# First layer of a long network on one Trainium2 core: sums of weights with a vector moved from GpSimd and VectorE to TensorE

## The chip, the cores and the metric

One program runs on one core of a Trainium2 chip. The metric is the device time of one execution in microseconds (us); less is better. The engines are TensorE (PE in the profile; PEld is its loading of weights), VectorE (DVE), ScalarE (ACT), GpSimd (POOL) and SyncE (SP, which here issues the DMAs). Each takes its own instructions in order and waits for the others by semaphores.

## The reference

A network over 512 tokens of width 1024, in float32. Only its first layer matters here, for the latents x and for a context ctx of 256 tokens:

```python
s_lat, s_ctx = silu(c), silu(c_ctx)                        # vectors of 1024
mod_l = split(s_lat @ ada_w[0] + ada_b[0], 6)              # shift, scale, gate; shift, scale, gate
mod_c = split(s_ctx @ ada_w[0] + ada_b[0], 6)
a_lat = rmsnorm(x, norm1_g[0]) * (1 + mod_l[1]) + mod_l[0]
a_ctx = rmsnorm(ctx, norm1_g[0]) * (1 + mod_c[1]) + mod_c[0]
p_lat = a_lat @ mix_w_in + mix_b_in                        # q, k, v and the hyena columns
kv_ctx = a_ctx @ mix_w_in[:, 512:1536] + mix_b_in[512:1536]
att = differential_attention(q, [k_ctx, k], [v_ctx, v])    # 4 heads, 512 queries, 768 keys
hy = x0 * long_conv(v * x1)                                # from the hyena columns
x = x + mod_l[2] * (concat(att, hy) @ mix_w_out + mix_b_out)
x = x + mod_l[5] * (relu(modulate(rmsnorm(x), mod_l[3], mod_l[4]) @ w1) ** 2 @ w2)
```

Behind it come a second layer (pooling and another MLP) and two layers of another kind (recurrence, attention, gated feed-forward).

## The kernel before

**Products.** Features lie on the partitions, tokens on the free axis. Every large product is made of three passes in a fast float32 form: weights and inputs are each split into a rounded part h and a remainder l, and `mm3` (lines 456 to 460) adds wh·xh, wl·xh and wh·xl into a PSUM bank. A tile of the product over 1024 rows is 24 matmuls of 128x512.

**Stream of weights.** Weights arrive in parts of 512 KB in a ring of six `raw` buffers (`_dma_to`, L233). `_emit_h` makes h on ACT (L255) and `_emit_l` makes l on DVE or POOL (L273); then the buffer is free, and SP issues the DMA of the part six places on. `consume` hands out a part for a product, and before it returns calls `prefetch(look)`, which emits the splits of the parts beyond. Parts of the modulation weights `ada_w` (kind "ada") are mixed into this stream; they are not split. `plan` (L742) sets the order: behind the last k part two such parts, behind the pairs of `qh` parts 4, 2, 4, 2, 4, 4 and 2.

**Sums of weights with a vector.** The vectors of modulation are sums over the rows of `ada_w`, each row times an entry of `s_lat`. `_ada_step` (L386) multiplies each raw 128x512 block by a scalar per partition on POOL (L371) or ACT (L373) and adds it on POOL (L383) to an accumulator; when the eight blocks of a half are through, DVE transposes and reduces (`ada_sums`, L416 and L418), and `flush` puts the entries on their partitions by TensorE (L426). A half is 512 of the 6144 entries; halves 0 and 1 are the first shift, 2 and 3 the scale, 4 to 11 the rest.

**Order of the first layer.** `start` (0 to about 140 us) computes V of x and ctx from inputs times gains, in eight steps k; the gains are small TensorE products (`strip`, L1007). `first_shift` sums halves 0 and 1 for x and for ctx, a part at a time beside the steps k (`fstep`): half 0 on POOL, half 1 on DVE (L369, L378) and on ACT with POOL. The sums over the partitions are 32 TensorE instructions (L1096), and the shift `sh` follows (L1099). Then the normed inputs A and AC are made (L1112 to L1136). `layer0` goes on with q (one tile), four k tiles for x and ctx (about 130 to 184 us), and 16 steps s of attention (to about 375 us). In each step the scores of 128 queries (L1492, L1497), the softmax, the combination of two components (L1519, L1520), transposes (L1533) and the product with V stand beside one tile of the `qh` columns. The long convolution and the output product end the layer's mixing at about 475 us. `v_shift`, run in steps beside the k tiles and the first attention steps, multiplies the raw V weights by the shift: for x on DVE (L369, L378), for ctx on ACT and POOL (L373, L383), then a TensorE sum over the partitions (L1161).

**PSUM.** Six banks (`ps`) serve the products and two (`pss`) the small ones: strips, transposes, sums.

Of the kernel before, what the change touches and what calls it, by code (L numbers as in the profile page):

```python
# [11 lines left out]
F32 = mybir.dt.float32  # L12
# [42 lines left out]
class Weights:  # L55
    """h and l views of one part, by chunk of the contraction"""
# [9 lines left out]
# which engine takes which small operation, and the order of the steps that run beside each other  # L66
# [10 lines left out]
    ada='GGAGGA',  # L77
    fs='GGVA',
    vs='VA',
    fstep=(1, 2, 1, 0, 0, 1, 0, 3),  # L80
# [29 lines left out]
    vsj=(2, 1, 0, 1),  # L110
    fj=(1, 2, 0, 2),
    vs1=(0, 1, 1, 1, 1, 1, 1, 1, 1, 1, 1, 1, 1, 1, 1, 1),
    vs2=(1, 1, 0, 3, 1, 1, 1, 1, 1, 1, 1, 1, 1, 1, 1, 1),
# [22 lines left out]
class Prog:  # L136
    def __init__(self, tc, ctx, a, out, tap=None):
# [23 lines left out]
        self.look = LOOK  # L161
        self.l_eng = self.V
# [33 lines left out]
    def piece(self, label, src, parts):  # L196
        """src: dram view, rows x blocks x columns; parts: (kind, which blocks and columns of the view, extra), each loaded alone"""
        for kind, (k, n), extra in parts:
            p = dict(label=label, src=src[:, k, n], raw=None)
            self.pieces.append(p)  # L200
            self.parts.append((p, (kind, extra)))

    def wpiece(self, label, w, k0, kc, n0, nc_, by_k=False, shift=None):
        """shift: (layer, which) of the shift whose product with the weights is wanted besides"""
# [112 lines left out]
    def prefetch(self, n_ahead):  # L317
        """splits emitted up to n_ahead weight parts beyond the one consumed last"""
# [23 lines left out]
    def consume(self, label):  # L342
# [15 lines left out]
        self.prefetch(self.look)  # L358
        return W

# [5 lines left out]
    def scaled(self, mode, out, x, sc):  # L366
        """out = x * sc, by the vector engine, by GpSimd or by the scalar engine"""
        if mode == "V":
            self.V.tensor_scalar(out, x, sc, None, op0=ALU.mult)  # L369
        elif mode == "G":  # L370
            self.G.tensor_scalar(out, x, sc, 0.0, op0=ALU.mult, op1=ALU.add)  # L371
        else:
            self.S.activation(out, x, AF.Copy, scale=sc)  # L373

    def add_scaled(self, mode, out, x, sc):
        """out += x * sc, by the vector engine, by GpSimd or by the scalar engine and GpSimd"""
# [9 lines left out]
    def _ada_step(self, p, layer, half, i):  # L386
        raw = p["raw"]
        s = self.s_lat if layer < 2 else self.col("c_2", 0, 8)
        mode = (PR["ada"][half - 4] if layer == 0 and 4 <= half < 10 else self.ada_mode)
# [14 lines left out]

    def ada_tick(self, want=None):
        """the rest of sums that came ready a while ago, or of those wanted"""
# [14 lines left out]
    def flush_into(self, out, src):  # L421
        """A column of ada_r holds 32 entries, each as the sums over the four quarters of the partitions: add these up
        and put each entry on its partition."""
# [4 lines left out]
    def flush(self, layer):  # L428
        """the modulation vectors that are ready"""
# [32 lines left out]
    def gemm(self, label, x, n_tiles, evac, outer=0, looks=None):  # L462
        """x: list of (h, l) tiles, one for each 128 of the contraction; evac(m, psum)"""
# [38 lines left out]
    def steps(self, gen):  # L502
        """one step of the generator with each tick"""
# [10 lines left out]
    def gemm1(self, label, xs):  # L514
# [4 lines left out]
        for k, x in enumerate(xs):  # L519
            self.mm3(ps[:], w[k], x, k == 0, k == len(xs) - 1)  # L520
        self.put(w.tiles)
# [73 lines left out]
    def head_x(self, k):  # L595
        """x times the norm's gains, ahead of the norm"""
# [8 lines left out]
    def head(self, chain, gs, sh, evac):  # L605
        """The first four tiles of a product with a norm's output start from x times the gains; the factor of each token
        and the product with the shift come on behind. chain() gives the factors. Returns the norm's output."""
# [43 lines left out]
    def norm_mod(self, xs, bc, gs, sh, n=T, free=False, each=None):  # L651
        """h/l pairs of x * rstd * gs + sh"""
# [32 lines left out]
    def gain(self, name, layer, i, g=None, width=8):  # L685
        """g * (1 + scale) as columns"""
# [9 lines left out]
    def sin_red(self, x, out, P, tmp, quarter=False):  # L696
        """out = sin(x), or cos(x); x is kept. In steps"""
# [84 lines left out]
    # parts split ahead by the last products before a norm: the head's parts are through before the last ones  # L782
# [73 lines left out]
    def hyena_filter(self, hd, w3):  # L856
        """Spectrum of the filter, in steps. With t and f both even or odd the transform falls into four of half the size:
        frequency 511 - f has the cosine and sine of f, but for signs that go by the parity of t."""
# [47 lines left out]
    def hyena_hidden(self, z, w1, w2, w3):  # L906
        """hidden layers of the filter's network, in steps"""
# [23 lines left out]
    def first_shift(self):  # L931
        """sums over the rows of the first layer's weights for the shifts of x and ctx, in steps"""
        for half in range(2):
            acc = [self.get(), self.get()]
            for i in range(4):
                p = self.parts[self.cur][0]
                self.cur_h = self.cur_l = self.cur = self.cur + 1
                for kk in range(2):
                    k = 2 * i + kk
                    for c, o in enumerate(acc):  # L940
                        sc, w = self.s2[:, k, c:c + 1], p["raw"][:, kk, :]
                        if k == 0:
                            self.scaled(PR["fs"][2 * half + c], o[:], w, sc)
                        else:
                            self.add_scaled(PR["fs"][2 * half + c], o[:], w, sc)
                self._done_part(p)
                if i == 3:
                    self.first_acc.append(acc)
                yield

    # steps of the filter's hidden layers, and strips of the gains, beside each part of V
# [3 lines left out]
    def start(self):  # L955
        """V of x and ctx, tokens on the partitions, from the tokens times the norm's gains: the factor of each token is put
        on it, the product with the shift is left to v_shift. Besides, the first layer's normalised inputs."""
# [38 lines left out]
        gg, sh = c.tile([128, 8, 2], F32, name="gg"), c.tile([128, 8, 2], F32, name="sh")  # L996
        b1 = c.tile([128, 8], F32, name="b1")
# [3 lines left out]
        hidden, shift, self.first_acc = self.hyena_hidden(z, w1, w2, w3), self.first_shift(), []  # L1001

        def strip(k):
            """128 of the gains of x and ctx, in steps"""
# [86 lines left out]
        ps = self.ps_s.tile([128, 512], F32, tag="pss", name="pss")  # L1091
        for half, acc in enumerate(self.first_acc):
            for c_, o in enumerate(acc):
                for k in range(4):
                    j = 8 * c_ + 4 * half + k
                    PE.matmul(ps[:, j:j + 1], lhsT=o[:, k * 128:(k + 1) * 128], rhs=self.ones[:, 0:1], start=True, stop=True)  # L1096
            self.put(acc)
        for c_ in range(2):
            V.tensor_tensor(sh[:, :, c_], ps[:, 8 * c_:8 * c_ + 8], self.col("ada_b", 0, 8), op=ALU.add)  # L1099
# [40 lines left out]
        self.sh = sh  # L1140
# [5 lines left out]
    def v_shift(self):  # L1146
        """V's products with the shifts, in steps; then V's parts"""
        V, G, S = self.V, self.G, self.S
        acc = [self.get(), self.get()]
        for k in range(8):  # L1150
            for c, o in enumerate(acc):
                if k == 0:
                    self.scaled(PR["vs"][c], o[:], self.vw[k][:], self.sh[:, k, c:c + 1])
                else:
                    self.add_scaled(PR["vs"][c], o[:], self.vw[k][:], self.sh[:, k, c:c + 1])
            self.put(self.vw[k])
# [1244 lines left out]
```

## Time and profile before

| | us |
|---|---|
| median of 3 runs (lowest, highest) | 2698.91 (2698.41, 2698.95) |
| span of the profiled execution | 2697.1 |
| PE, DVE, ACT, POOL busy | 2487.8, 1863.4, 1106.0, 1567.3 |
| mean granted TensorE clock | 0.952 |

The span is that of the profiled execution, from its first to its last instruction; the runs' median lies 1.8 us above it. Clock 1.00 is TensorE's higher level, 2.4 GHz; 0.50 is 1.2 GHz. A busy PE need not be PE at its peak, and a matmul's recorded duration includes its drain; the distance between two starts shows its cost in a stream.

### The profile page before, as it was taken

What the parts mean: (1) busy time and instruction counts of PE and PEld (TensorE: products, weight loads), DVE (VectorE), ACT (ScalarE), POOL (GpSimd) and SP (SyncE); (2) the same over time, 40 slices, a digit from 0 to 9 for tenths busy, and PEclk for the clock granted to TensorE, in tenths of its full rate; (3) what the DMA queues carried; (4) which work ended last, traced back from release to release, by engine and by line L of the source; (5) the groups of instructions that cost most, each with busy time, mean ns of one, the idle gap of its engine ahead of it and who ended that gap; (6) DMA issues with size and microseconds to landing.
All of it is one profiled execution on the core that took longest, in us unless ns stands there. A gap on an engine that the chain in (4) does not pass through costs nothing.

```text
span 2697.1 us, 32008 instructions
## 1 busy us (share of the span) xinstructions
PE 2487.8 (92%) x11472; PEld 2068.4 (77%) x11472; DVE 1863.4 (69%) x2612; ACT 1106.0 (41%) x2057; POOL 1567.3 (58%) x1250
## 2 busy tenths in 40 slices
PE   7787778999989899999879999999999799999998
PEld 6665667787868688888668887888877688788887
DVE  6899988776666787766888667455477876733334
ACT  3446553433223433334466543222245654423231
POOL 6687756699981689963675348778146744400001
PEclk8788989999989899999889999999999899999999
DMA  7233332366673167662312235666422123233331
GB/s 244 83 118 102 109 94 86 95 191 199 200 218 97 51 177 210 213 177 72 96 57 67 87 92 164 182 192 201 117 75 81 49 81 117 71 102 94 95 91 50
DMA packets 433368, 330.30 MB, mean 122 GB/s; under 512 B 11799, under 2 KB 365207, under 8 KB 433208
## 3 DMA queue, kind: packets, MB, share of 16 engines
q1 hardware_dynamic: 429976, 322.22, 39.8%
q0 software_dynamic: 3232, 6.03, 0.7%
q8 instruction: 90, 1.47, 0.2%
q14 instruction: 70, 0.57, 0.1%
HBM read 319.82 MB, written 8.39 MB: 122 GB/s over the span
## 4 chain that ended last, share of the span: by engine, by line
PE 52%; DVE 8%; POOL 3%; ACT 2%; issue 2%; POOLq 0%; DVEq 0%; ACTq 0%
PE ps L458 16%; PE ps L460 16%; PE ps L459 16%; PE ps L477 2%; PE ps L619 1%; POOL slot L273 1%; DVE slot L1973 1%; POOL slot L664 1%; DVE slot L1925 1%; DVE slot L2038 1%; DVE slot L1961 1%; DVE slot L527 1%; PE ps L2029 0%; DVE slot L682 0%; PE pss L574 0%
## 5 line engine op out<-in xcount | busy, mean ns | idle before, releaser
L458 PE MATMUL ps<-slot 128*128 128x512 f32 (+2 forms) x3120 | 1209.2, 388 | 56.0 <-DVE slot L527 16.8
L460 PE MATMUL ps<-slot 128*128 128x512 f32 (+2 forms) x3120 | 1202.8, 386 | 45.8 <-DVE slot L682 24.7
L459 PE MATMUL ps<-slot 128*128 128x512 f32 (+2 forms) x3120 | 1200.8, 385 | 16.6 <-DVE slot L273 13.5
L458 PEld LDWEIGHTS ps<-slot 128*128 128x128 f32 x3120 | 603.4, 193 | 174.1 <-DVE slot L527 19.6
L460 PEld LDWEIGHTS ps<-slot 128*128 128x128 f32 x3120 | 602.4, 193 | 169.0 <-DVE slot L682 32.7
L459 PEld LDWEIGHTS ps<-slot 128*128 128x128 f32 x3120 | 602.9, 193 | 128.9 <-DVE slot L273 15.2
L255 ACT CAST slot<-raw 128x512 fp32r<-128x512 f32 (+1 forms) x764 | 425.8, 612 | 339.6 <-DMA raw<-in_mlp_w_dram 220.2
L383 POOL TENSOR_TENSOR slot<-slot 128x512 f32<-128x512 f32 x336 | 489.9, 1458 | 57.9 <-ACT slot L373 30.5
L273 DVE TENSOR_TENSOR slot<-raw,slot 128x512 fp32r<-128x512 f32 (+1 forms) x554 | 486.9, 922 | 36.7 <-ACT slot L255 32.0
L542 POOL TENSOR_TENSOR slot<-slot 128x512 f32<-128x512 f32 (+1 forms) x64 | 88.0, 1380 | 555.7 <-ACT slot L536 550.1
L273 POOL TENSOR_TENSOR slot<-raw,slot 128x512 fp32r<-128x512 f32 (+1 forms) x210 | 307.7, 1490 | 141.0 <-ACT slot L255 100.1
L371 POOL TENSOR_SCALAR slot<-raw,cols 128x512 f32<-128x512 f32 x192 | 206.1, 1076 | 58.0 <-DMA raw<-in_w_ada_dram 39.7
L371 POOL TENSOR_SCALAR slot<-raw,s_lat 128x512 f32<-128x512 f32 x144 | 154.9, 1079 | 6.4 <-DMA raw<-in_ada_w_dram 6.3
L619 PE MATMUL ps<-slot 128*128 128x512 f32 x576 | 145.5, 412 | 7.4 <-DVE slot L1812 7.4
L2187 DVE TENSOR_TENSOR slot<-slot,ps 128x512 f32<-128x512 f32 x40 | 27.5, 687 | 175.5 <-PE ps L460 175.5
L536 ACT ACTIVATE slot<-slot 128x512 f32<-128x512 f32 (+1 forms) x98 | 55.3, 575 | 214.4 <-DVE slot L1708 61.4
L619 PEld LDWEIGHTS ps<-slot 128*128 128x128 f32 x576 | 114.0, 200 | 32.5 <-DVE slot L1812 8.3
L526 ACT CAST slot<-slot 128x512 fp32r<-128x512 f32 x80 | 47.1, 619 | 190.0 <-DVE slot L2187 155.8
L664 POOL TENSOR_SCALAR slot<-slot,g,mod 128x512 f32<-128x512 f32 x48 | 57.2, 1198 | 85.8 <-DVE slot L658 85.8
L527 DVE TENSOR_TENSOR slot<-slot 128x512 fp32r<-128x512 f32 x75 | 81.7, 1110 | 35.7 <-ACT slot L526 35.7
L2212 DVE SCALAR_TENSOR_TENSOR slot<-ps,mod,slot 128x512 f32<-128x512 f32 x40 | 30.0, 749 | 102.2 <-PE ps L460 102.2
L416 DVE STREAM_TRANSPOSE slot<-slot 128x512 f32<-128x512 f32 x44 | 31.1, 706 | 94.7 <-POOL slot L383 94.6
(322 smaller groups left out, 2796.7 us busy)
## 6 DMA issues: line engine op xcount, KB each, us to landing
raw<-in_mlp_w_dram SPq DMA_DIRECT2D x128, 512.0 KB, 4.8
raw<-in_w_ada_dram SPq DMA_DIRECT2D x96, 512.0 KB, 4.4
raw<-in_ada_w_dram SPq DMA_DIRECT2D x88, 512.0 KB, 5.0
raw<-in_w_ffn_in_dram SPq DMA_DIRECT2D x88, 512.0 KB, 4.2
raw<-in_w_in_dram SPq DMA_DIRECT2D x56, 512.0 KB, 3.8
raw<-in_w_ffn_out_dram SPq DMA_DIRECT2D x32, 512.0 KB, 5.3
raw<-in_mix_w_dram SPq DMA_DIRECT2D x20, 512.0 KB, 3.9
raw<-in_w_out_dram SPq DMA_DIRECT2D x16, 512.0 KB, 4.1
```

Of the source, the lines that this page charges most:

```text
L255: self.S.copy(r(v), src[:, k:k + kk, :])
L273: eng.tensor_tensor(r(lv), src, v, op=ALU.subtract)
L371: self.G.tensor_scalar(out, x, sc, 0.0, op0=ALU.mult, op1=ALU.add)
L383: self.G.tensor_tensor(out, out, v, op=ALU.add)
L458: self.PE.matmul(out, lhsT=wh, rhs=xh, start=start, stop=False)
L459: self.PE.matmul(out, lhsT=wl, rhs=xh, start=False, stop=False)
L460: self.PE.matmul(out, lhsT=wh, rhs=xl, start=False, stop=stop)
L527: (eng or self.V).tensor_tensor(r(l)[:, 0:n], src, h[:, 0:n], op=ALU.subtract)
L536: self.S.activation(sq[:, 0:n], x, AF.Square, scale=scale)
L542: (eng or self.G).tensor_tensor(st["acc"][:, 0:n], st["acc"][:, 0:n], sq[:, 0:n], op=ALU.add)
L619: PE.matmul(ps[:], lhsT=w[i][:, m * 128:(m + 1) * 128], rhs=r(x[j])[:], start=(k == 0 and n == 0), stop=(k == 7 and n == 2))
L664: self.G.tensor_scalar(y[:, 0:n], t[:, 0:n], gs[:, k:k + 1], sh[:, k:k + 1], op0=ALU.mult, op1=ALU.add)
```

## The change

The sums of the first layer with a vector are computed by TensorE in plain float32 from the raw blocks: a raw block is the stationary operand (128 columns at a time), the vector one or two moving columns. This holds for the first shift (halves 0 and 1), for halves 4 to 9, and for V's product with the shift, where the shift, broadcast to 128 columns, is stationary and the raw V weights move. In the first layer `prefetch` is called behind the matmuls of the product that consumed a part, not ahead of them. `fetch_late` ends where the output product begins. The orders `fstep`, `vsj` and `vs2` change with it; docstrings and comments are taken out.

```diff
-    ada='GGAGGA',
-    fs='GGVA',
-    vs='VA',
-    fstep=(1, 2, 1, 0, 0, 1, 0, 3),
+    fstep=(0, 1, 1, 0, 2, 2, 2, 0),
-    vsj=(2, 1, 0, 1),
+    vsj=(0, 1, 0, 1),
-    vs2=(1, 1, 0, 3, 1, 1, 1, 1, 1, 1, 1, 1, 1, 1, 1, 1),
+    vs2=(0, 1, 0, 3, 1, 1, 1, 1, 1, 1, 1, 1, 1, 1, 1, 1),
...
+        self.fetch_late = True
...
         W = p["hl"].pop(id(part))
         self.cur += 1
-        self.prefetch(self.look)
+        if not self.fetch_late:
+            self.prefetch(self.look)
         return W
+
+    def fetch(self):
+
+        if self.fetch_late:
+            self.prefetch(self.look)
...
     def _ada_step(self, p, layer, half, i):
         raw = p["raw"]
         s = self.s_lat if layer < 2 else self.col("c_2", 0, 8)
-        mode = (PR["ada"][half - 4] if layer == 0 and 4 <= half < 10 else self.ada_mode)
+        if layer == 0 and half < 10:
+            m, b = self.mod[0][:, half * 4:half * 4 + 4], self.col("ada_b", half * 4, 4)
+            ps = self.columns(raw, self.s_lat, 2 * i, 1)
+            self.V.tensor_tensor(m, ps, b if i == 0 else m, op=ALU.add)
+            if i == 3:
+                self.ready.add((layer, half))
+            return
+        mode = self.ada_mode
...
+    def columns(self, raw, vec, k0, n):
+
+        ps = self.ps_s.tile([128, 512], F32, tag="pss", name="pss")
+        for j in range(4):
+            for kk in range(2):
+                self.PE.matmul(ps[:, n * j:n * j + n], lhsT=raw[:, kk, j * 128:(j + 1) * 128],
+                               rhs=vec[:, n * (k0 + kk):n * (k0 + kk) + n], start=(kk == 0), stop=(kk == 1))
+        return ps[:, 0:4 * n]
...
@@ gemm1
             self.mm3(ps[:], w[k], x, k == 0, k == len(xs) - 1)
+        self.fetch()
         self.put(w.tiles)
...
     def first_shift(self):
+        s2 = self.s2[:].rearrange("p k c -> p (k c)")
+        for c in range(2):
+            self.V.tensor_copy(self.sh[:, :, c], self.col("ada_b", 0, 8))
         for half in range(2):
-            acc = [self.get(), self.get()]
+            o = self.sh[:, 4 * half:4 * half + 4, :].rearrange("p k c -> p (k c)")
             for i in range(4):
                 p = self.parts[self.cur][0]
                 self.cur_h = self.cur_l = self.cur = self.cur + 1
-                for kk in range(2):
...
+                self.V.tensor_tensor(o, o, self.columns(p["raw"], s2, 2 * i, 2), op=ALU.add)
                 self._done_part(p)
-                if i == 3:
-                    self.first_acc.append(acc)
                 yield
...
@@ start, behind the eight steps
-        ps = self.ps_s.tile([128, 512], F32, tag="pss", name="pss")
-        for half, acc in enumerate(self.first_acc):
...
-                    PE.matmul(ps[:, j:j + 1], lhsT=o[:, k * 128:(k + 1) * 128], rhs=self.ones[:, 0:1], start=True, stop=True)
-            self.put(acc)
-        for c_ in range(2):
-            V.tensor_tensor(sh[:, :, c_], ps[:, 8 * c_:8 * c_ + 8], self.col("ada_b", 0, 8), op=ALU.add)
...
     def v_shift(self):
-        acc = [self.get(), self.get()]
-        for k in range(8):
-            for c, o in enumerate(acc):
...
-        for c, o in enumerate(acc):
-            ps = self.ps_s.tile([128, 512], F32, tag="pss", name="pss")
-            self.PE.matmul(ps[:], lhsT=self.ones[:], rhs=o[:], start=True, stop=True)
-            V.tensor_tensor(o[:], ps[:], self.bv[:], op=ALU.add)
+        V, acc = self.V, []
+        for c in range(2):
+            ps, o = self.ps_s.tile([128, 512], F32, tag="pss", name="pss"), self.get()
+            for k in range(8):
+                self.PE.matmul(ps[:], lhsT=self.sh[:, k, c:c + 1].to_broadcast([128, 128]), rhs=self.vw[k][:],
+                               start=(k == 0), stop=(k == 7))
+            V.tensor_tensor(o[:], ps[:], self.bv[:], op=ALU.add)
+            acc.append(o)
+            if c == 0:
+                yield
+        self.put(self.vw)
         self.put(self.bv)
...
@@ layer0, the k tiles
                 self.mm3(pc[:, 0:TC], w[k], acs[k], k == 0, k == 7)
+            self.fetch()
...
-        self.look = 0
+        self.look, self.fetch_late = 0, False
```

## Rows read from the trace of the kernel before

**Rows 1.** Busy time by stretch: length, each engine, clock, DMA share, GB/s.
```profile
0.00:88.30 88.30, 69.44 (x307) 57.25 (x308) 65.55 (x97) 29.17 (x56) 56.83 (x51) 0.86 0.64 215
88.30:99.30 11.00, 6.46 (x40) 6.13 (x39) 7.16 (x8) 5.12 (x10) 4.72 (x3) 0.68 0.56 164
...
130.10:184.40 54.30, 42.49 (x201) 35.28 (x202) 53.64 (x67) 26.87 (x47) 46.01 (x32) 0.85 0.35 114
184.40:240.70 56.30, 39.11 (x164) 31.11 (x164) 50.53 (x71) 31.90 (x71) 38.28 (x31) 0.83 0.24 77
240.70:304.00 63.30, 56.60 (x284) 46.77 (x284) 60.88 (x103) 36.94 (x89) 47.71 (x42) 0.93 0.42 133
304.00:375.00 71.00, 56.46 (x286) 47.45 (x284) 63.41 (x111) 43.86 (x97) 36.48 (x28) 0.93 0.29 89
375.00:440.00 65.00, 47.05 (x258) 41.16 (x259) 57.85 (x97) 21.37 (x41) 48.25 (x36) 0.84 0.28 90
```

**Rows 2.** What PE waited for, 130.1 to 304 us: total, times, longest.
```profile
PE pss L1533 <- DVE slot L1520: 13.2, 3, 10.5
```

**Rows 3.** POOL's groups by line, 130.1 to 304 us: busy us, mean ns.
```profile
L383 POOL TENSOR_TENSOR slot<-slot 128x512 f32<-128x512 f32 x40 | 59.5, 1487 | 11.5 <-ACT slot L373 8.5
L371 POOL TENSOR_SCALAR slot<-raw,s_lat 128x512 f32<-128x512 f32 x30 | 31.2, 1043 | 0.0
```

**Rows 4.** DVE in order of time, one operation before and beside POOL's sums.
```profile
20.62 0.42 DVE L700 TENSOR_SCALAR slot<-slot 64x512 f32<-64x512 f32 x1
...
41.11 1.37 DVE L700 TENSOR_SCALAR slot<-slot 64x512 f32<-64x512 f32 x1
```

**Rows 5.** DVE's groups by line and shape, 140 to 200 us.
```profile
L378 DVE SCALAR_TENSOR_TENSOR slot<-slot,sh 128x512 f32<-128x512 f32 x7 | 9.6, 1372 | 0.2
```

**Rows 6.** The same, 200 to 310 us.
```profile
L416 DVE STREAM_TRANSPOSE slot<-slot 128x512 f32<-128x512 f32 x4 | 2.8, 702 | 0.0
L418 DVE TENSOR_REDUCE ada_r<-slot 128x16 f32<-128x512 f32 x4 | 2.7, 685 | 0.1
```

**Rows 7.** All engines in order of time, 76 to 135 us: start, length.
```profile
88.04 7.50 DVE L378 SCALAR_TENSOR_TENSOR slot<-raw,s,slot 128x512 f32<-128x512 f32 x6
...
91.54 3.46 POOL L273 TENSOR_TENSOR slot<-raw,slot 128x512 fp32r<-128x512 f32 x2 [0.68 <-ACT slot L255]
...
95.59 3.58 PE L1096 MATMUL pss<-ones,slot 128*128 128x1 f32 x16 [4.08 <-DVE slot L378]
...
100.23 4.32 POOL L1122 TENSOR_SCALAR slot<-slot,gg,sh 128x512 f32<-128x512 f32 x2 [5.23 <-DVE slot L1112]
```

**Rows 8.** PE in order of time, 190 to 194.5 us.
```profile
191.50 1.88 PE L1161 MATMUL pss<-slot,ones 128*128 128x512 f32 x4
192.82 1.49 PE L1492 MATMUL ps<-slot 128*128 128x512 f32 x4
```

**Rows 9.** PE in order of time, 1600 to 1618 us: a norm's sums inside a head.
```profile
1605.96 1.84 PE L574 MATMUL pss<-ones,slot 128*128 128x1 f32 x16
1607.66 1.03 PE L629 MATMUL pss<-ones,slot 128*128 128x1 f32 x8
1608.55 3.03 PE L619 MATMUL ps<-slot 128*128 128x512 f32 x12
```

**Rows 10.** The same in another head, 1252 to 1276 us.
```profile
1259.74 3.84 PE L574 MATMUL pss<-ones,slot 128*128 128x1 f32 x32
1263.44 1.84 PE L629 MATMUL pss<-ones,slot 128*128 128x1 f32 x8
1265.15 5.17 PE L619 MATMUL ps<-slot 128*128 128x512 f32 x12
```

**Rows 11.** PE's busy time and granted clock in that head, by us.
```profile
1262.00:1263.00 1.00, 1.00 (x11) 1.00 0.00 0
1263.00:1264.00 1.00, 1.00 (x7) 0.50 0.00 0
```

**Rows 12.** The page's DMA issues: KB each, us to landing.
```profile
raw<-in_ada_w_dram SPq DMA_DIRECT2D x88, 512.0 KB, 5.0
```

More of the change, by code (lines that the diff above doesn't have):

```diff
@@ L937, in first_shift @@
                 self.cur_h = self.cur_l = self.cur = self.cur + 1
-                for kk in range(2):
-                    k = 2 * i + kk
-                    for c, o in enumerate(acc):
[L941 to L945, printed above, removed]
+                self.V.tensor_tensor(o, o, self.columns(p["raw"], s2, 2 * i, 2), op=ALU.add)
                 self._done_part(p)
-                if i == 3:
-                    self.first_acc.append(acc)
                 yield
@@ L996, in start @@
         gg, sh = c.tile([128, 8, 2], F32, name="gg"), c.tile([128, 8, 2], F32, name="sh")
+        self.sh = sh
         b1 = c.tile([128, 8], F32, name="b1")
@@ L1000, in start @@
         gx, gc, ws = [], [], []
-        hidden, shift, self.first_acc = self.hyena_hidden(z, w1, w2, w3), self.first_shift(), []
+        hidden, shift = self.hyena_hidden(z, w1, w2, w3), self.first_shift()
         def strip(k):
@@ L1090, in start @@
         S.copy(rc[:, 0:TC], bp[:, 0:TC])
-        ps = self.ps_s.tile([128, 512], F32, tag="pss", name="pss")
-        for half, acc in enumerate(self.first_acc):
-            for c_, o in enumerate(acc):
-                for k in range(4):
-                    j = 8 * c_ + 4 * half + k
-                    PE.matmul(ps[:, j:j + 1], lhsT=o[:, k * 128:(k + 1) * 128], rhs=self.ones[:, 0:1], start=True, stop=True)
-            self.put(acc)
-        for c_ in range(2):
-            V.tensor_tensor(sh[:, :, c_], ps[:, 8 * c_:8 * c_ + 8], self.col("ada_b", 0, 8), op=ALU.add)
         self.vt = []
@@ L1139, in start @@
         self.put(rc)
-        self.sh = sh
         self.put(cxt)
@@ L1146, in v_shift @@
     def v_shift(self):
-        V, G, S = self.V, self.G, self.S
-        acc = [self.get(), self.get()]
-        for k in range(8):
-            for c, o in enumerate(acc):
[L1152 to L1156, printed above, removed]
-            if k % 2:
+        V, acc = self.V, []
[7 more added lines that the diff above has]
+            if c == 0:
                 yield
-        for c, o in enumerate(acc):
-            ps = self.ps_s.tile([128, 512], F32, tag="pss", name="pss")
-            self.PE.matmul(ps[:], lhsT=self.ones[:], rhs=o[:], start=True, stop=True)
-            V.tensor_tensor(o[:], ps[:], self.bv[:], op=ALU.add)
+        self.put(self.vw)
         self.put(self.bv)
```

## The prediction

> **What bounds the kernel now.** I read the busy times by stretch first [rows 1], for the change touches only the first 440 us. There DVE is busy nearly all the time from 130.1 to 440 us (286.3 of 309.9 us), PE less: between 130.1 and 304.0 us, the stretch of the last three k tiles and steps 0 to 9, PE is busy 138.2 of 173.9 us, at a mean clock of 0.83 to 0.93. Next came PE's waits in that stretch: the longest are the transposes' for the combination on DVE [rows 2]. So in the first layer the end is set by DVE, in its order, and PE fills in. Third, I looked at what keeps DVE: the same operation on 64x512 takes 0.42 us while POOL is silent and 1.37 us while POOL sums weights [rows 4]. POOL's sums (L383 and L371) are 90.7 us of that stretch [rows 3], and the change takes nearly all of them away. This speaks for the change. Last, I asked of PE what it must now take, and at which clock; that decides my forecast.
>
> **What PE has to do between 130.1 and 304.0 us.** Busy time by clock gives the work at the full clock: 42.49 by 0.85, 39.11 by 0.83 and 56.60 by 0.93 make 36.1 + 32.5 + 52.6 = 121 us [rows 1]. So PE has some 53 us in hand there, as waits and as time at the lower clock.
>
> Added is, first, V's product with the shift: 16 products of 128x512 in plain float32. Two such products (four instructions) stand in the trace of before: 1.32 us to the start of the next group, 1.88 us with the drain [rows 8], so a product costs between 0.66 and 0.94 us. I take 0.85, nearer the upper end, as the group behind starts slowly. 16 by 0.85 less the two removed is 11.9 us.
>
> Second, the modulation: 24 parts, 22 of them in this stretch (behind the last k part and the pairs of qh parts; the last 2 fall in step 11, behind 304 us). A part is 8 products with one moving column, which are 16 instructions. Sixteen such instructions lie in a norm: 1.70 us from the first to the start of the next group [rows 9]. 22 by 1.70 is 37.4 us. Together 121 + 11.9 + 37.4 = 170 us: the stretch would be full to the brim, against 173.9 us before, with no wait left.
>
> **The clock.** The parts come in bunches, by the order of the stream two w parts ahead of the product: 4 behind the last k tile and in steps 3, 7 and 9; 2 behind the second k tile and in steps 1 and 5. A bunch of 4 is 64 one-column instructions, 6.8 us in which hardly a column moves. What such a run does is seen in the heads of the later layers. In one, 40 of them stand together, PE is busy without a gap, and yet the granted clock falls from 1.00 to 0.50 after 3.3 us [rows 11]; the twelve 512-column matmuls behind them take 5.17 us instead of 3.03 [rows 9, 10]. Of the six heads in the trace, five with 24 of these instructions and one with 40, the clock fell in five. So I expect it to fall in every bunch of 4 and in most of the bunches of 2.
>
> The price: in the head with 40, the twelve matmuls cost 2.1 us more and the eight instructions before them 1.71 us (start to start) instead of 0.89, together 3.0 us. A bunch of 4 has 24 instructions more, at the lower clock, each 0.10 us dearer (1.71 less 0.89, over eight): 2.4 us more. I take 5 us for each of four bunches of 4 and 1.5 us for each of three bunches of 2 (between nothing, as in the one head that was spared, and 3.0): 20 + 4.5 = 24.5 us. Bounds: 0 (no fall) and 31 us (5.4 and 3.0).
>
> The Trainium skill states the opposite for such a run: by its page "TensorE: Matmul & The Clock Gate", section "Why this matters for your kernels", throughput drops come from idle gaps between bursts and an occupied PE keeps its higher clock. By that rule the 24.5 us would be nothing; the head's rows do not agree with it, and the sum goes by them. It is the first rival below.
>
> Waits that stay: PE will still wait for DVE at the start of a head of attention and when a bunch meets DVE's other work, for a third part needs the bank of the first, and its addition stands behind the splits (L273) in DVE's order. I take 3 us of the 35.7 us idle of before; bounds 0 and 12. Stretch: 170 + 24.5 + 3 = 198 us, that is **+24 us**.
>
> **What DVE gives back there** is hidden: it loses the sums of V's shift (L378, 9.6 us and one operation more [rows 5]), transposes and reductions of the halves (5.5 us [rows 6]) and much of POOL's interference, and gains 24 small additions. DVE had 165 of 173.9 us; with these gone and a third of its slow operations quick again it needs some 120 to 135 us, an estimate from those rows. It is no longer the bound, and what it gains is worth only the waits that I have already taken out of PE's sum. An addition waits for the product ahead of it on PE; behind it on DVE stand the maxima of the next scores, which PE makes later anyway, so this costs nothing as long as PE is the bound.
>
> **The start, 0 to 130.1 us.** Removed: the sums of the first shift on three engines. The last ones on DVE run to 95.5 us, the 32 PE instructions to 99.2 us, and the first normed input on POOL starts at 100.2 us [rows 7]. After it the shift is there early. What is late next is POOL's own queue: the split of the q part (91.5 to 95.0 us) stands ahead of that first operation, so the gain is 5.2 us if that split stays in place and at most 11 us (the whole stretch from 88.3) if it moves up by as much. Added are 8 parts on PE, 13.6 us, in a stretch where PE has 18.9 us idle up to 88.3 us [rows 1], waiting mostly for DVE, which is relieved of POOL. I take these two as cancelling, with bounds of -4 and +8 (bunches of 2 lower the clock here too). The start: **-5 us**, bounds -11 and +3.
>
> **The tail, 304 to 440 us.** DVE is busy 121 of 136 us [rows 1]. It loses two transposes and two reductions (2.8 us by the means of [rows 6]) and a little interference; PE gains 3.4 us, where it has 32 us idle. **-4 us**, bounds -7 and 0.
>
> **Edits at no cost.** `prefetch` behind the product changes the order on PE alone, since splits run on other engines: without it each bunch would wait for its DMA ahead of a product. Raw buffers are now freed by PE at a part's end, and SP's queue, which keeps its order, then issues the part six places on: at least one whole product lies between, and a landing takes 5.0 us [rows 12]. Were that cover gone, it would be up to 5 us for each late bunch. `vsj` and `vs2` follow from `v_shift`'s fewer steps.
>
> **Sum.** 24 - 5 - 4 = +15 us on the profiled 2697.1 us gives 2712; the runs' median lies 1.8 us above the span, so **2714 us** (+0.55%).
>
> **Rivals.**
> 1. *The clock holds* (the rule above): the stretch costs 170 + 3 against 173.9, so -1; with the start and the tail -10, and DVE's bounds give up to -20. Time 2689 us (2679 to 2693). For it: the one spared head [rows 9]. Against it: five heads of six. The sign turns where the falls cost 10 us in all, 2 us for a bunch of 4. Chance 0.31: this is the case on the other side.
> 2. *The falls are half as dear*, or partly hidden where PE waits anyway: 12 us in the place of 24.5, so +2, within 0.2% of before: 2701 us (2694 to 2704). Chance 0.17. (0.2%, 5.4 us, is about what a measurement of this kernel can tell from no change.)
> 3. *Two banks are too few*: each third and fourth part of a bunch waits for DVE, whose queue is late. Ten such waits of 1 to 2 us on top: 2729 us. For it: one DVE operation takes 1.37 us when disturbed [rows 4]; against it: DVE gets time. Chance 0.09.
> The forecast has 0.43 (2705 to 2724). Faster 0.31, same 0.17, slower 0.43 + 0.09 = 0.52. The range that holds 8 in 10 takes in most of rivals 1 and 3: 2683 to 2727; the forecast's own is 2705 to 2724.
>
> **What would show it.** Right: between the k tiles and step 10 PE idle nearly gone, its clock at 0.50 behind each bunch of 4, 16 instructions of a part in 1.7 us (about 3.4 at the lower clock), the stretch near 198 us; POOL nearly silent there, DVE's operations near their undisturbed time, with DVE waiting for PE; the normed inputs starting some 5 us earlier; all behind 475 us unchanged. Wrong: a clock near 1.00 through the bunches (rival 1), or DVE still full in the stretch, which would mean that the interference was not POOL's sums.

## The result and the profile after

The changed kernel takes 2724.99 us (median of 4 runs, 2723.25 to 2725.86) against 2698.66 us before: ratio 1.0096, interval 1.0082 to 1.0109. It is slower, on the side that was forecast: 11 us above the forecast's 2714, 1 us outside its own range (2705 to 2724) and inside the range that holds 8 in 10 (2683 to 2727). The profiled execution has a span of 2722.5 us, 25.4 more than before.

To compare the two traces I cut both at the same places of the program: at the end of the first k tile (its 24 products with the context, 256 columns each), at the end of the fourth group of 18 attention products (behind step 9), and at the last products of 256 columns, where the layer's output product has begun. First the busy times by stretch of the changed kernel (length, then PE, PEld, DVE, ACT and POOL, PE's granted clock, DMA share, GB/s):

```profile
0.00:128.83 128.83, 111.88 (x519) 92.64 (x519) 76.96 (x140) 47.28 (x89) 37.79 (x38) 0.83 0.51 168
128.83:334.53 205.70, 201.93 (x1028) 174.64 (x1027) 129.00 (x252) 89.80 (x197) 44.94 (x35) 0.85 0.33 105
334.53:455.60 121.07, 98.36 (x541) 85.70 (x539) 101.56 (x184) 57.44 (x125) 59.86 (x46) 0.89 0.25 79
455.60:2722.50 2266.90, 2155.03 (x9889) 1792.40 (x9888) 1476.66 (x2041) 892.14 (x1616) 1270.74 (x1014) 0.97 0.41 122
```

and of the kernel before, cut at the same places ([rows 1] have other edges):

```profile
128.93:304.16 175.23, 138.75 (x647) 113.32 (x647) 166.38 (x241) 97.04 (x211) 132.16 (x103) 0.87 0.34 108
304.16:433.10 128.94, 97.84 (x516) 83.82 (x515) 115.14 (x196) 64.45 (x137) 77.67 (x59) 0.88 0.30 94
433.10:2697.10 2264.00, 2153.36 (x9889) 1791.51 (x9888) 1482.23 (x2038) 892.12 (x1616) 1270.64 (x1015) 0.97 0.41 123
```

The start is as long as before (128.8 against 128.9 us), the stretch 30.5 us longer, the tail 7.9 us shorter, and what lies behind 2.9 us longer. In the stretch PE is busy for 201.9 of 205.7 us, DVE for only 129.0, and POOL's 132 us have become 45. DVE was relieved as expected: here are the combination's first operation, the splits of the weights and the rope's operation on 64 rows, after and then before (busy us, mean ns):

```profile
L1522 DVE SCALAR_TENSOR_TENSOR slot<-slot,rc 128x512 f32<-128x512 f32 x9 | 7.3, 814 | 0.3
L271 DVE TENSOR_TENSOR slot<-raw,slot 128x512 fp32r<-128x512 f32 x30 | 23.6, 829 | 0.1
L1438 DVE TENSOR_TENSOR slot<-slot 64x512 fp32r<-64x512 f32 x6 | 4.1, 686 | 0.1
```

```profile
L1519 DVE SCALAR_TENSOR_TENSOR slot<-slot,rc 128x512 f32<-128x512 f32 x9 | 12.5, 1388 | 0.3
L273 DVE TENSOR_TENSOR slot<-raw,slot 128x512 fp32r<-128x512 f32 x28 | 26.7, 992 | 0.1
L1435 DVE TENSOR_TENSOR slot<-slot 64x512 fp32r<-64x512 f32 x6 | 8.5, 1414 | 0.1
```

That it was POOL's sums that slowed them is shown by e1 (below), which gives POOL its sums of the modulation back and keeps V's shift on TensorE; there the combination's first operation is as slow as before:

```profile
L1516 DVE SCALAR_TENSOR_TENSOR slot<-slot,rc 128x512 f32<-128x512 f32 x9 | 12.5, 1385 | 0.3
```

What PE was given instead, by line, and its one wait of more than 1 us in the stretch (before, 13.2 us in one row alone [rows 2]):

```profile
L421 PE MATMUL pss<-s_lat,raw 128*128 128x1 f32 x352 | 53.6, 287 | 3.0 <-issue 2.9
L1158 PE MATMUL pss<-slot,sh 128*128 128x512 f32 x32 | 14.1, 592 | 0.0
...
PE pss L421 <- issue: 2.9, 1, 2.9
```

And the clock in one bunch of four parts, PE in order of time and then its busy time and granted clock over the same microseconds:

```profile
176.88 10.39 PE L421 MATMUL pss<-s_lat,raw 128*128 128x1 f32 x64
187.20 0.58 PE L1188 MATMUL pss<-lampr,ones 64*128 64x2 f32 x2
187.71 0.80 PE L478 MATMUL ps<-slot 128*128 128x512 f32 x1
188.30 0.63 PE L479 MATMUL ps<-slot 128*128 128x512 f32 x1
188.73 0.63 PE L480 MATMUL ps<-slot 128*128 128x512 f32 x1
```

```profile
176.80:180.40 3.60, 3.60 (x36) 1.00 0.26 68
180.40:187.20 6.80, 6.80 (x34) 0.50 0.69 220
187.20:190.60 3.40, 3.40 (x10) 0.50 0.52 154
190.60:194.80 4.20, 4.20 (x20) 0.99 0.00 0
```

PE has no gap here. The first half of the run goes at 2.4 GHz (36 records in 3.6 us), then the granted clock is 0.50, which is 1.2 GHz; the wide products behind start 0.43 us apart in place of 0.23, until it rises. It is what the head of a later layer showed [rows 10, 11].

### The profile page after: what moved, and what is told of

It is laid out like the page before. It is cut to its first block, busy times and chain, and to the rows that moved or that the text cites. A ratio compares the mean times of both kernels' runs of the same rounds, so it can differ in the third digit from the quotient of the medians.

```text
span 2722.5 us, 32842 instructions
## 1 busy us (share of the span) xinstructions
PE 2567.2 (94%) x11972; PEld 2145.4 (79%) x11972; DVE 1784.2 (66%) x2615; ACT 1086.7 (40%) x2025; POOL 1413.3 (52%) x1132
## 4 chain that ended last, share of the span: by engine, by line
PE 50%; DVE 8%; POOL 3%; ACT 2%; issue 2%; DMA 0%; SPq 0%; POOLq 0%; DVEq 0%; ACTq 0%
PE ps L478 15%; PE ps L480 15%; PE ps L479 15%; PE ps L497 1%; PE ps L640 1%; POOL slot L271 1%; DVE slot L1976 1%; POOL slot L685 1%; DVE slot L1928 1%; DVE slot L2041 1%; DVE slot L1964 1%; DVE slot L548 1%; DVE slot L679 0%; DVE slot L703 0%; PE ps L2032 0%
## 5 line engine op out<-in xcount | busy, mean ns | idle before, releaser
L271 DVE TENSOR_TENSOR slot<-raw,slot 128x512 fp32r<-128x512 f32 (+1 forms) x554 | 476.5, 904 | 38.1 <-ACT slot L253 34.7
L387 POOL TENSOR_TENSOR slot<-slot 128x512 f32<-128x512 f32 x266 | 387.0, 1455 | 22.2
L375 POOL TENSOR_SCALAR slot<-raw,s_lat 128x512 f32<-128x512 f32 x112 | 122.6, 1097 | 6.5 <-DMA raw<-in_ada_w_dram 6.4
```

The costliest lines, as they stand in the source:

```text
L271: eng.tensor_tensor(r(lv), src, v, op=ALU.subtract)
L387: self.G.tensor_tensor(out, out, v, op=ALU.add)
```

## The experiments

Every kernel was cut at the same three places. "Work" is PE's busy time in each window of 1 us times the clock granted in that window, summed over the stretch: what PE would need at the full clock. "Clock" is the rest of its busy time, "idle" what is left of the stretch. Times are medians; the columns behind them come from each kernel's one profiled execution, which lies up to 8 us off its median (e11). The kernels e1 to e4, e5 to e8 and e9 to e12 each ran beside the kernel before, whose medians there were 2698.9, 2700.4 and 2698.4 us; the ratios are to these, so across these groups compare the ratios.

| kernel | us | ratio to before (interval) | start | stretch = work + clock + idle | tail |
|---|---|---|---|---|---|
| before | 2698.7 | | 128.9 | 175.2 = 124.9 + 13.9 + 36.5 | 128.9 |
| changed | 2725.0 | 1.0096 (1.0082 to 1.0109) | 128.8 | 205.7 = 171.4 + 30.5 + 3.8 | 121.1 |
| e1_mod_back | 2686.1 | 0.9956 (0.9945 to 0.9968) | 126.9 | 168.7 = 135.6 + 9.9 + 23.2 | 128.6 |
| e2_rows | 2715.9 | 1.0063 (1.0049 to 1.0078) | 132.1 | 196.2 = 178.8 + 7.1 + 10.3 | 121.2 |
| e3_fetch_ahead | 2755.5 | 1.0212 (1.0190 to 1.0234) | 121.7 | 233.8 = 172.0 + 42.1 + 19.8 | 128.5 |
| e4_first_shift_back | 2724.6 | 1.0105 (1.0082 to 1.0128) | 129.1 | 210.0 = 171.0 + 34.4 + 4.7 | 121.9 |
| e5_rows_late | 2722.8 | 1.0088 (1.0076 to 1.0100) | 120.0 | 205.2 = 178.0 + 10.9 + 16.3 | 124.3 |
| e6_spread | 2708.5 | 1.0039 (1.0026 to 1.0052) | 126.6 | 193.0 = 171.8 + 18.9 + 2.3 | 121.6 |
| e7_v_shift_alone | 2693.8 | 0.9977 (0.9968 to 0.9985) | 128.3 | 170.0 = 135.0 + 12.6 + 22.5 | 129.0 |
| e8_two_halves | 2703.6 | 1.0005 (0.9993 to 1.0018) | 130.5 | 176.4 = 151.3 + 9.0 + 16.1 | 128.1 |
| e9_singles | 2697.0 | 0.9996 (0.9982 to 1.0009) | 128.8 | 179.5 = 164.8 + 11.9 + 2.7 | 124.3 |
| e10_half_singles | 2681.4 | 0.9932 (0.9919 to 0.9945) | 125.6 | 167.8 = 151.4 + 9.2 + 7.2 | 122.1 |
| e11_back_singles | 2690.4 | 0.9965 (0.9951 to 0.9979) | 124.4 | 171.2 = 135.0 + 12.5 + 23.7 | 126.0 |
| e12_back_late | 2689.9 | 0.9964 (0.9952 to 0.9976) | 133.1 | 168.8 = 135.5 + 10.0 + 23.3 | 128.6 |

### Which part costs: modulation, V's shift or first shift

**e1** puts the modulation's sums back, and with them the fetch ahead of the product:

```
-        if layer == 0 and half < 10:
-            m, b = self.mod[0][:, half * 4:half * 4 + 4], self.col("ada_b", half * 4, 4)
-            ps = self.columns(raw, self.s_lat, 2 * i, 1)
...
+        mode = (PR["ada"][half - 4] if layer == 0 and 4 <= half < 10 else self.ada_mode)
...
-        self.fetch_late = True
+        self.fetch_late = False
```

> The modulation goes back to the vector sums on GpSimd, ScalarE and VectorE, with the fetch ahead of the product; the two shifts stay on TensorE. Theory (the modulation's one-column products are what lengthens the stretch of the last three k tiles and steps 0 to 9, by their own 40 us and by the falls of the clock behind them): the stretch returns to being VectorE's, less the sums of V's shift (about 10 us of VectorE), and the two products of V's shift fit into TensorE's idle time: 2685 to 2696 us. Rival A (V's shift on TensorE is itself on the path, 14 us): 2705 to 2715 us. Rival B (the loss lies in the start, where TensorE makes the first shift): within 3 us of the changed kernel, 2722 to 2728 us.

Measured: 2686.1 us, faster than both kernels. All the loss was the modulation's (the place of the fetch, which changes too, matters little here: e12, below); the two shifts on TensorE are a gain. In the stretch:

```profile
126.90:295.60 168.70, 145.52 (x675) 116.81 (x675) 153.22 (x233) 93.59 (x204) 119.11 (x97) 0.92 0.35 113
...
PE pss L1530 <- DVE slot L1517: 12.7, 3, 10.1
PE ps L1489 <- DVE slot L1432: 6.3, 4, 2.6
```

PE took V's products and still waits 23 us, most of it for DVE, as before the change [rows 2].

**e4** puts only the first shift's sums back (`first_shift` and its 16 products with ones, 32 instructions, behind the norm), **e7** both these and the modulation's, so that V's shift alone is on TensorE.

> The first shift goes back to the vector sums, the rest stays changed. Theory (start: the earlier shift gains nothing, since the norm's small products come 6 us later behind TensorE's eight parts, which cancels the chain that was taken away): 2722 to 2728 us. Rival A (as forecast, the first shift on TensorE gains 5 us in the start): 2728 to 2733 us. Rival B (the first shift on TensorE costs): below 2720 us.

> Only the product of V with the shifts is on TensorE; the first shift and the modulation are vector sums as before. Theory (what made the kernel with the modulation put back 12.8 us faster is V's shift, which leaves VectorE in the stretch that it bounds; the first shift gives nothing): 2684 to 2692 us. Rival (the first shift on TensorE gives part of it, by the start): 2693 to 2699 us.

Measured: e4 as the changed kernel, 2724.6 us, so there the first shift gives nothing that can be seen, within an interval 12 us wide; e7 at 2693.8 us, above its theory's range and inside its rival's, so V's shift alone gives some 6 us by the ratio, and the first shift seems to give part of the rest (e1 and e12, which differ from e7 by it, e12 by the place of the fetch too, are 3 to 6 us lower by their ratios, with intervals that touch or overlap). How much the first shift is worth stays open within that.

### Is it the clock?

**e2** makes the same multiplications with the operands exchanged: the block moves in 512 columns, the vector stands. A half's four rows are added on VectorE, and four one-column products turn the sum at the end.

```
-            ps = self.columns(raw, self.s_lat, 2 * i, 1)
-            self.V.tensor_tensor(m, ps, b if i == 0 else m, op=ALU.add)
+            ps = self.ps_s.tile([128, 512], F32, tag="pss", name="pss")
+            for kk in range(2):
+                k = 2 * i + kk
+                self.PE.matmul(ps[0:1, :], lhsT=self.s_lat[:, k:k + 1], rhs=raw[:, kk, :], start=(kk == 0), stop=(kk == 1))
...
+            self.V.tensor_tensor(acc[0:1, :], ps[0:1, :], acc[0:1, :], op=ALU.add)
```

> The modulation stays on TensorE with the same multiplications, but the blocks move and the vector stands: two products of 1x512 a part, the row summed on VectorE, and four one-column products for each half at its end. A part is then as long as before in TensorE's time (V's shift shows 0.88 us a product, 1.76 us a part against 1.81). Theory (the granted clock falls behind the one-column runs and takes 25 to 30 us of the stretch): the granted clock stays at 1.00 there and the time falls by 15 to 25 us, to 2700 to 2710 us. Rival A (the clock falls for another reason, such as plain f32 work in itself): clock as before, 2722 to 2728 us. Rival B (the two banks or VectorE's additions, now 0.7 us each, are what binds): TensorE waits in the bunches, 2720 us or more.

The stretch, and its longest wait:

```profile
132.10:328.30 196.20, 185.92 (x804) 123.17 (x803) 139.43 (x257) 89.75 (x197) 43.91 (x35) 0.96 0.35 108
...
PE pss L409 <- DVE slot L404: 6.2, 5, 2.5
```

The mean clock is 0.96 in place of 0.85, and the time lost to it 7.1 us in place of 30.5: no bunch loses the clock, and it falls only behind waits. So the falls belonged to the one-column runs. Of these 23 us, 7.4 went into more work, most of it the turning at the halves' ends, and 6.5 into waits, most of them for VectorE's last addition; 9 us are left in the median, less than I expected: 2715.9 us lies above the theory's 2700 to 2710.

**e5** puts the turning two products later:

```
+                def turn():
...
+                self.defer(turn, 2)
```

> As the kernel with the moving blocks (2716 us), but the four one-column products at a half's end come two products later, not at once behind VectorE's last addition. There TensorE waited 6.2 us in five places for that addition, and the clock fell behind two of these waits (7 us lost to the lower clock in the stretch). Theory (what is left over the kernel before is TensorE's own work, 54 us more than before in the stretch): waits and falls go, the work stays: 2703 to 2711 us, still slower than before. Rival (with the falls gone TensorE is no longer the bound and the time comes down to that of before): 2700 us or less.

It missed: 2722.8 us. The wait did not go, it moved and grew:

```profile
PE pss L411 <- DVE slot L1566: 13.5, 3, 9.2
```

The turning now stands where both banks of the pool hold transposed attention weights that VectorE still has to split. So two banks can bind, if a step stands in the wrong place (e3, below, shows it too).

**e6** leaves the columns as they are and changes only the order of the stream, so that a bunch of four becomes two of two, and one of two becomes two of one; **e9** puts one part behind each of the k and qh parts, two behind five of them.

```
+            ws, ad = self.parts[n0:n1], self.parts[n1:]
+            c = len(ad) // 2
+            self.parts[n0:] = ws[:1] + ad[:c] + ws[1:] + ad[c:]
```

```
+        for i, e in enumerate(ws):
+            c = 2 if i in (4, 7, 10, 13, 16) else 1
+            mixed += [e] + ad[:c]
+            ad = ad[c:]
```

> The changed kernel with its columns, but each bunch of four modulation parts is put as two of two, and each of two as two of one, by the order of the stream alone. Same work, same operations. Theory (the clock falls by the length of a run of one-column products; a fall came 2 to 5 us after the start of a run): runs of one part, 1.8 us, are spared, runs of two fall in part; the time lost to the lower clock in the stretch falls from 30 to between 10 and 22 us: 2704 to 2718 us. Rival (the fall does not go by the length of the run, each run of any length pays one): as many runs more, 2725 to 2740 us.

> All shifts and the modulation on TensorE by columns, as in the changed kernel; the 24 modulation parts are put one behind each of the k and qh parts (two behind five of them), by the order of the stream alone. In the kernel with bunches of two and one, all six bunches of one in or behind the stretch were spared, and seven of eight bunches of two saw the clock fall. Theory (the fall goes by the length of the run): the time lost to the lower clock in the stretch falls from 18.9 to 5 to 10 us: 2694 to 2702 us, the time of the kernel before, at which TensorE's own work is what is left. Rival (runs of one 6 us apart are seen as one): 2705 to 2713 us.

Measured: 2708.5 and 2697.0 us, both inside the theory's ranges. The order alone gives back the 26 to 28 us of the change. In e6, a single part with the products around it, and then a pair with those behind it (busy time, clock):

```profile
200.00:206.00 6.00, 6.00 (x38) 1.00 0.46 139
217.30:219.60 2.30, 2.30 (x23) 1.00 0.00 0
219.60:225.90 6.30, 6.30 (x29) 0.52 0.75 212
225.90:229.00 3.10, 3.10 (x15) 0.87 0.28 79
```

From the first k tile on, the clock fell in all four bunches of four and three of four pairs of the changed kernel, in seven of nine pairs of e6 and in none of its six singles; in e9 in four of five pairs, and one single of twelve stood at the lower clock, behind a wait of 2.7 us for a bank. (The expectation of e9 counts one pair too few.) e9's clock still takes 11.9 us, by four pairs and that wait, more than the 5 to 10 us of the theory. Its work is 6.6 us lower because two parts have moved ahead of the stretch and two more behind it.

### Where the part is fetched

**e3** is the changed kernel with `self.fetch_late = False`.

> The changed kernel with the parts fetched ahead of the product, as in the kernel before. Theory (without its cover each bunch waits for a raw block or stands ahead of a product that could run): 0 to 15 us slower, 2725 to 2740 us. Rival (fetching behind the product has no use; the order does not matter to a TensorE that is full anyway): 2722 to 2728 us.

It is 30 us slower still, twice what I allowed:

```profile
121.70:355.50 233.80, 214.02 (x1028) 184.26 (x1027) 125.98 (x252) 89.63 (x197) 43.60 (x35) 0.80 0.30 93
...
PE pss L421 <- issue: 17.1, 4, 9.1
```

PE stands for 16 us more, mostly in four waits ahead of bunches, and the clock, which also falls in such waits, takes 11.6 us more. The table of waits names no releaser ("issue"). The theory took a raw block for it; all engines in order of time show another. Two of the four places, and the one wait of the changed kernel:

```profile
263.72 1.03 PE L1536 MATMUL pss<-ident,slot 128*128 128x128 f32 x8
267.89 1.28 DVE L1548 TENSOR_TENSOR slot<-pss,slot 128x512 fp32r<-128x512 f32 x2
268.68 1.61 PE L421 MATMUL pss<-s_lat,raw 128*128 128x1 f32 x7 [2.08 <-issue]
...
291.72 1.04 PE L1536 MATMUL pss<-ident,slot 128*128 128x128 f32 x8
297.59 1.28 DVE L1548 TENSOR_TENSOR slot<-pss,slot 128x512 fp32r<-128x512 f32 x2
298.38 1.96 PE L421 MATMUL pss<-s_lat,raw 128*128 128x1 f32 x13 [3.79 <-issue]
```

```profile
239.30 1.28 DVE L1548 TENSOR_TENSOR slot<-pss,slot 128x512 fp32r<-128x512 f32 x2
240.08 4.24 PE L421 MATMUL pss<-s_lat,raw 128*128 128x1 f32 x27 [2.90 <-issue]
```

PE's transposes fill both banks of the pool; DVE splits them some microseconds later, and each time the bunch starts 0.15 us after the first of the two splits has ended (half of the 1.28 us of the pair); in the other two places of e3 it is 0.14 us. So it waits for a bank. A bunch ahead of the product meets the transposes just made; behind the product DVE has had its 5.6 us. That it is the bank is read from these times; no run with a third bank was made.

### How much of the modulation to move

**e8** takes e1, puts the first two halves on TensorE (by moving blocks, the turning as in e5) and fetches behind the product; **e10** has the order of e9 with halves 4, 6 and 8 by columns and the others as vector sums; **e11** is that order with all six as vector sums, **e12** is e1 with `self.fetch_late = True`.

```
-        if layer == 0 and half < 10:
+        if layer == 0 and half in (4, 6, 8):
...
-        mode = self.ada_mode
+        mode = (PR["ada"][half - 4] if layer == 0 and 4 <= half < 10 else self.ada_mode)
```

> Both shifts and two of the six modulation halves (the first eight parts) on TensorE, these with moving blocks; four halves stay vector sums; fetch behind the product. Theory (TensorE has 23 us idle in the stretch, mostly in waits for VectorE near these parts; eight parts cost it 15 us and relieve GpSimd and so VectorE there): 2674 to 2686 us, faster than with none. Rival (TensorE's work adds to the path part for part): 2690 to 2702 us.

> The same order, but only halves 4, 6 and 8 of the modulation are on TensorE, by columns; 5, 7 and 9 are vector sums. Theory (the stretch is bounded by the fuller of TensorE and VectorE, and three halves fill both evenly: TensorE's work at the full clock about 153 us, and VectorE with half of GpSimd's interference): 2676 to 2688 us, at or below the kernel with no modulation on TensorE. Rival (as with two halves, what TensorE takes on adds to the path): 2692 to 2704 us.

> The same order, both shifts on TensorE, all six halves of the modulation as vector sums, fetch behind the product. Theory (the order matters only through TensorE's runs): as with the modulation put back and its old order, 2682 to 2690 us. Rival (evenly spread sums disturb VectorE in other places): beyond this either way.

> The modulation put back, its old order, but the fetch behind the product. Theory (where to fetch matters only to parts that TensorE sums, since it waits for their blocks): 2683 to 2690 us. Rival (fetching behind the product delays the splits of the weights, and this is what the kernel with two halves lost): 2693 to 2703 us.

e8 missed: 2703.6 us, above both ranges. Of the work that it adds, PE's idle time should have taken the most, but 9.3 us of that time are now a wait of the turning itself for a bank:

```profile
PE pss L412 <- DVE slot L1567: 9.3, 1, 9.3
```

e10 is the fastest of all, 2681.4 us, 0.68% under the kernel before and 9 us under e11 and e12, with which it ran. Its stretch and its tail:

```profile
125.60:293.40 167.80, 160.58 (x834) 134.64 (x835) 137.47 (x246) 90.32 (x197) 80.79 (x65) 0.94 0.37 111
293.40:415.50 122.10, 98.64 (x525) 84.47 (x523) 106.90 (x183) 62.33 (x133) 70.43 (x53) 0.86 0.31 94
```

The same 16 us of work that e8 added are taken here by idle time (23.3 us in e12, 7.2 here), so the stretch is as long as e12's. Where the 9 us come from, the profiles show only in part. The two profiled executions are 8 us apart: e10's start is 7.5 us shorter, its stretch 1.0 and its tail 6.5, and what lies behind is 7.0 longer. The start and what lies behind vary by as much from kernel to kernel without a cause in the code (below), so only the tail's gain, which the changed kernel has too, can be named, and against e11 the tail is 3.9 us shorter. e11 and e12 lie within 3 us of e1 by their ratios, and their executions overlap with e1's (e11 is 0.4 us above its range): neither the order nor the place of the fetch matters much to parts that TensorE does not sum.

## Why the prediction came right, and where it was off

**The stretch, forecast +24, measured +30.5 us.** Its three terms held: PE's work at the full clock 171.4 us (170 forecast), the clock 30.5 (24.5), waits 3.8 (3). The agreement in work is in part luck. The work of before is 124.9 us by windows of 1 us, not the 121 that I took from the mean clocks of long stretches, which count idle time too. What was added is as forecast: counted from each start to the next, at the full clock, the 22 parts take 38.4 us (37.4 forecast), and V's products less the two removed 11.6 (11.9). But PE's other work came out 3.4 us lower than before, 2.2 of them in the scores and the transposes; that less of their drain counts as busy where no wait follows is my reading, which no run tests. The term that was mis-sized is the clock. Added up over windows of half a microsecond, the four bunches of four lost 5.1, 6.8, 5.1 and 3.4 us, 20.4 together against 20 forecast; the three of two 3.4, 3.4 and 0, together 6.8 against 4.5. One bunch of four and two of two cost more than my bounds of 5.4 and 3.0. The last 3.3 us are a fall at the stretch's head, behind the waits of the start: I had let all falls of before vanish with PE's waits, and this one stayed.

**That the clock is the cause** was argued from the heads of the later layers and is now shown from two sides: other operands for the same sums (e2), and the same operations in another order (e6, e9). Rival 1, that it holds in a run without gaps, falls: the run from 176.9 to 187.2 us has no gap and stands at 0.50 from 180.4 us on. By the Trainium skill, page "TensorE: Matmul & The Clock Gate", section "Why this matters for your kernels", drops of throughput come from idle gaps between bursts of products. That run does not agree, and the measurement decides. The rival's condition came nearest in e9, where the clock takes 11.9 us of the stretch, and there the time is 2697.0 us, not 2689: what stays is the start, which gave little, and that part of the clock's price.

**DVE's relief is hidden**, as forecast: 129.0 us busy, in the middle of 120 to 135, and of no use while PE is full. e1 shows the other side: with the modulation off PE, DVE is busy for 153.2 of 168.7 us, 13 us less than before, and the stretch is 6.5 us shorter than before.

**The start, forecast -5, measured -0.1 us.** The step that failed is that eight parts on PE and DVE's relief cancel. PE's work there rose by 9.7 us and its clock took 19.5 us in place of 15.1. The norm's own small products then stand behind the last part:

```profile
81.71 3.92 PE L421 MATMUL pss<-s,raw 128*128 128x2 f32 x32
85.49 2.70 PE L1097 MATMUL pss<-ones,slot 128*128 128x1 f32 x12
94.65 0.82 PE L584 MATMUL pss<-ident,ny 128*128 128x128 f32 x6
97.90 3.21 POOL L271 TENSOR_TENSOR slot<-raw,slot 128x512 fp32r<-128x512 f32 x2
101.09 2.24 POOL L1129 TENSOR_SCALAR slot<-slot,gg,sh 128x512 f32<-128x512 f32 x1
```

The factors of the tokens are on the partitions at 94.65 us, where before it was 88.29:

```profile
88.29 0.82 PE L563 MATMUL pss<-ident,ny 128*128 128x128 f32 x6
```

That is 6.4 us late, and the chain that was taken away had cost as much. The split of the q part stayed ahead of the first normed input, as said, which starts at 101.09 against 100.23 us [rows 7]. One execution settles a term of 5 us here only roughly: eight kernels with the changed start end it between 120.0 and 133.1 us (last section), 127.5 in the mean, and the three with the old one (before, e4, e7) at 128.3 to 129.1. PE's work and idle time alone, without the clock's part, are 109.4 to 112.6 us in the eight, and 113.8, 119.2 and 113.0 in the three: so some 3 us or more are gained there as far as these show, and what the clock takes hides them.

**The tail, forecast -4, measured -7.9 us**, just past its bound of -7: VectorE's busy time fell by 13.6 us there, more than the transposes and reductions, because its operations are quicker there too (the combination's first takes 893 ns in the mean in place of 1132).

**Behind**, forecast 0, measured +2.9 us: PE's work is the same to 0.1 us; 1.8 is the clock and 1.2 idle time. That is within the scatter of this part: in the fourteen profiled executions it takes 2259.2 to 2269.3 us, with 2102 to 2104 us of work and 111 to 113 us idle in each, and 44.2 to 54.1 us lost to the lower clock.

**The fetch behind the product** was costed at nothing, with up to 5 us for each late bunch without it. e3 gives 30 us over seven bunches, 4.3 each, but for another reason than the one I gave: not the landing of a block, the banks.

**Rival 3**, two banks too few, has the right mechanism and the wrong size: in the changed kernel it costs one wait of 2.9 us, inside the 3 us that the sum allowed. Ahead of the product (e3), or with one more holder of a bank (e5, e8), it costs 17.1, 13.5 and 9.3 us of waits.

## What to carry to other kernels

Before sums move from a crowded engine to TensorE, add up TensorE's work at its full clock in that stretch: what is moved gains only as far as its idle time goes, and here half of the modulation fitted where all of it did not. Runs of one-column products cost more than their own time: put single ones between wide products, or let the wide operand move. And small sums that share a pool of banks with larger work belong where its banks have been emptied, here behind the product and not ahead of it.

## What was unexpected of the hardware

The start's length goes with the clock that it happens to be granted. Eight kernels with the same operations there (changed, e1, e2, e3, e5, e6, e8, e12; e1 and e3 fetch earlier at its end) have 92 to 94 us of work and 17 to 19 us idle in it, but lose 19.5, 16.2, 21.1, 10.9, 8.3, 16.2, 17.9 and 21.3 us to the lower clock, and end it at 128.8, 126.9, 132.1, 121.7, 120.0, 126.6, 130.5 and 133.1 us. What lies behind the tail varies in the same way, by 10 us (above). That is as much as most edits here are worth. The executions of one kernel differ by as much (e8: 2692.6 to 2708.4 us), more than those of the kernel before; that it is the clock there too is likely (e8's mean granted clock is 0.960 in its fastest execution, 0.954 in its slowest), but one execution of each kernel was profiled, so it is not shown.
